# A two-layer hybrid backbone on one core: recurrence levels in blocks, and a fixed TensorE order in the second mixer

## The chip, the core and the metric

The kernel runs on one core of a Trainium2 chip. The core has TensorE (PE in the profile; PEld is its loading of weights), VectorE (DVE), ScalarE (ACT), GpSimd (POOL) and SyncE (SP), which issues most DMAs. They share SBUF; matrix products go to PSUM, a small memory of eight banks that ACT and DVE empty. The metric is device time in microseconds, the median of several runs.

## What is computed

Two transformer-like layers over 512 latent tokens and 256 context tokens, of width 1024. Each layer has a mixer and a gated feed-forward network, each between norms that are scaled and shifted by a conditioning vector. The mixers hold a gated linear recurrence in both directions, and this is what the change is about:

```python
def _chunk_gla(q, k, v, g, s0):
    # S_t = diag(exp(g_t)) S_{t-1} + k_t v_t^T,  o_t = S_t^T q_t
    ...
def _directional_scan(q, k, v, g, n_ctx, reverse):
    o_ctx, s_ctx = _chunk_gla(seg(q, c_sl), seg(k, c_sl), seg(v, c_sl), seg(g, c_sl), s0)
    o_lat, _ = _chunk_gla(seg(q, t_sl), seg(k, t_sl), seg(v, t_sl), seg(g, t_sl), s_ctx)
```

The first mixer (`even_mixer`) has four heads of 64 keys and 128 values, for context and latents, beside an attention. The second (`odd_mixer`, HGRN2) has eight heads of 128 keys and 128 values. There q is silu of a projection, the forget gate f and the key 1 - f come from a sigmoid of another projection for each direction, only the latents' outputs are needed, and the context gives no more than the two starting states. The outputs are normed by head and multiplied by silu of a gate projection.

## The kernel before

Weights come by DMA in units of 128 x 1024 (`unit`, L447 to L459), and each is split in two parts, wH (ACT, L456) and wL (DVE, L457), so that a product is three TensorE passes (`mm3`, L463: L466, L467, L468). `gemm_T` gives a projection with tokens along the free axis; `gemm_nat` gives one with tokens on partitions. Three units of raw weights and four of each split part are in flight, so loads run ahead of their use.

A recurrence is done by `scan` (from L642) without a loop over time. The tile `arr` holds four rows: key and query for one direction, key and query for the other. For block sizes b = 1, 2, 4, ... 64 one level does this: ACT copies the halves that this level needs from `arr` to `qk` (L698, one copy of 128 x 1024 for both directions), DVE multiplies the running decays into one half of `arr` for each direction (L713, twice), and DVE forms the decays of the next level (L714). For b up to 16 a call of `compact` follows each copy: 16 small products of 32 x 32 blocks (`pc`, L675; 32 for the first mixer's longer pieces), which DVE merges by a mask into `CT` (L687). Before the levels one `compact` does the diagonal (evacuated by ACT, L685). Levels 32 and 64 give products of 64 x 64 blocks (`pb`, L731), which ACT copies to `ST` (L739) and DVE completes from `CT` (L742). Then, for each direction, the keys are transposed (`knp`, L757) and copied (`kn`, L758), multiplied with the values (`pd`, L762), and three updates give the states at the tile borders (L768, L770). Last come the output products (`po`, L784) and their evacuation by a function of the caller.

The first mixer calls `scan` in `gla_job` for two pairs of heads, each for the context and for the latents, in a list of steps (`"q kv qk0 v0 c0 prep l0 qk1 v1 g0 c1 r0 l1"`).

In the second mixer, `prep(hd)` makes a head's operands: for each direction the product `ff` (256 context columns, then 512), the sigmoid (L1174), the gates (L1178, L1180) and keys (L1179, L1181) by DVE, a running product over the context (L1186 or L1191), and then the product `fq`. The function `state` transposes the context's keys (`kcT`, L1199), copies them (L1201), and multiplies them with the values to the starting state (`S`, L1204). Then DVE forms q, the two decayed queries and the sum of keys (L1218 to L1221). `head` runs `scan` and norms the output (L1230 to L1236). The program goes

```python
            ready = prep(0)
            for hd in range(8):
                nxt = prep(hd + 1) if hd < 7 else None
                ...
                head(hd, *ready)
```

with three of four gate products (`gate`) ahead of the last head and one behind it.

The order on each engine isn't that of the program text: a planner in the framework takes instructions by their place in the program and by when it reckons them ready, and writes one fixed order for each engine. So the small products of a head stand between the wide products of the next. `keep_in_program_order` is the call that takes an instruction out of this choice. Tiles with a tag share a ring of buffers; a tile waits until the one that held its buffer is done with. PSUM has two "mm" tiles (two banks each, for wide products), two "sc" tiles that are taken in turn (`pc`, `pb`, `pd`, `S`), and two "tr" tiles (transposes and `po`). `qk` has four buffers.

Of the kernel before, what the change touches and what calls it, by code (L numbers as in the profile page):

```python
# [133 lines left out]
class Net:  # L134
# [3 lines left out]
    def __init__(self, ctx, tc, I, out):  # L138
# [3 lines left out]
        self.whole = False  # L142
        self.turns = []
# [10 lines left out]
    def open_pool(self, name, side="left"):  # L154
        return self.tc.alloc_tile_pool(name=name, bufs=1, side=side, reuse_waits="tile")

# [41 lines left out]
    def col_rows(self, nm, r0, r1, parts):  # L198

        rows = self.wp.tile([P, WU], F32, tag="mraw", bufs=2, name=nm)[: r1 - r0, :P]  # L200
        for at, src, n in parts:
            self.nc.scalar.dma_start(out=rows[at - r0 : at - r0 + n, :], in_=src)
        pt = self.tr_tile(f"pt_{nm}")
        self.nc.tensor.transpose(pt[:, 0 : r1 - r0], rows, self.ident[0 : r1 - r0, 0 : r1 - r0])
        self.nc.vector.tensor_copy(self.col[:, r0:r1], pt[:, 0 : r1 - r0])
# [56 lines left out]
    def mod_cols(self, l, acc, n, outs):  # L262
# [6 lines left out]
        for b in range(nb):  # L269
            last = nc.tensor.transpose(pt[:, b * P : (b + 1) * P], rows[:, b * P : (b + 1) * P], self.ident)  # L270
# [10 lines left out]
    def mod_group(self, l, ms, which=None, pool=None, bufs=2):  # L281
# [5 lines left out]
        for k in range(KD):  # L287
            us = self.mod_loads(l, ms, k, pool, bufs)
            for j in range(4):
                self.nc.tensor.matmul(  # L290
# [9 lines left out]
    def mod_vec(self, pool, jobs, own=None, bufs=2):  # L300
# [7 lines left out]
        for l, ms, then in jobs:  # L308
# [19 lines left out]
            for j in range(4):  # L328
                nc.tensor.matmul(
# [28 lines left out]
    def gate_rows(self, l, m, row, streams=2):  # L358
# [7 lines left out]
        nc.tensor.transpose(pt[0:n, 0:P], gc.rearrange("p r k -> p (r k)"), self.ident)  # L366
# [28 lines left out]
    def pre_norm(self, pool, t, xt, A, B, h):  # L395
# [8 lines left out]
        def turn():  # L404
            for hf in range(2):
# [3 lines left out]
                for kk in range(4):  # L409
                    k = hf * 4 + kk  # L410
                    nc.tensor.transpose(pt[:, kk * P : (kk + 1) * P], xn[:, k * P : (k + 1) * P], self.ident)
# [51 lines left out]
    def mm3(self, out, stat, mov, first, last):  # L463

        mm = self.nc.tensor.matmul
# [86 lines left out]
    def seven(self, W, h, X, fill, then=None):  # L552
# [5 lines left out]
        for wn, hn, x in SEVEN:  # L558
# [5 lines left out]
            for k in range(4):  # L564
                for i, (a, b) in enumerate(((wH, hH), (wH, hL), (wL, hH))):
                    nc.tensor.matmul(  # L566
# [75 lines left out]
    def scan(self, pool, nm, arr, q, ksum, dscale, f, nt, hpp, V, Sf0, Sb0, final, o_evac):  # L642
# [25 lines left out]
        def compact(lhs, rhs, m):  # L668
            for hh in range(hpp):
                pc = self.sc_tile(f"pc{nm}")  # L670
                pv = pc[:, : nt * 32].rearrange("p (s i) -> p s i", s=nt)
                for t in range(nt):
                    for j in range(4):
                        cs = slice(t * P + 32 * j, t * P + 32 * j + 32)
                        nc.tensor.matmul(  # L675
                            pv[32 * j : 32 * j + 32, t, :],
                            lhs[rowp(hh), cs],
                            rhs[rowp(hh), cs],
                            start=True,
                            stop=True,  # L680
                            tile_position=(rowt(hh), 32 * j),
                        )
                dst = CT[:, hh * nt : (hh + 1) * nt, :]
                if m is None:
                    nc.scalar.mul(dst, pv, dscale)  # L685
                else:
                    nc.vector.copy_predicated(dst, self.masks[:, m, :][:, None, :].to_broadcast([P, nt, 32]), pv)  # L687

        compact(ksum, q, None)

        b = 1
        while b < P:
            qk = pool.tile([P, 2, N], F32, tag="qk", bufs=4, name=f"qk{nm}{b}")
            src = arr[:, 0, :]
            inap = bass.AP(
                tensor=src.tensor, offset=src.offset, ap=[src.ap[0], [N, 2], [2 * b, N // (2 * b)], [2 * N + b, 2], [1, b]]
            )
            nc.scalar.copy(qk.rearrange("p a (n h o) -> p a n h o", h=2, o=b), inap)  # L698
# [5 lines left out]
            blk = arr.rearrange("p a (n h o) -> p a n h o", h=2, o=b)  # L704
            nb = N // (2 * b)
            tv = f[:, :, : 2 * nb].rearrange("p a (n h) -> p a n h", h=2)
            for lo, ohalf, thalf in ((0, 0, 1), (2, 1, 0)):
                dst = blk[:, lo : lo + 2, :, ohalf, :]
                tb = tv[:, :, :, thalf]
# [11 lines left out]
        for hh, t0, n in groups:  # L721
# [3 lines left out]
            for i in range(n):  # L725
                T0 = (t0 + i) * P
                for K, Q, x in ((K64, Q64, 1), (K32, Q32, 0)):
                    for j in range(2):
                        rs = slice(T0 + 64 * j, T0 + 64 * j + 64)
                        c0 = 64 * (j ^ x)  # L730
                        nc.tensor.matmul(  # L731
# [12 lines left out]

        states = [{}, {}]
        ends = []
        for d, S0, a in ((0, Sf0, 0), (1, Sb0, 2)):
            order = list(range(nt)) if d == 0 else list(range(nt))[::-1]
            steps = order if final else order[:-1]
            order = order + [None]  # L750
            kn = pool.tile([P, len(steps), P], F32, tag="kn", bufs=1 if hpp > 1 else 2, name=f"kn{nm}{d}")
            prev = S0
            if prev is not None:
                states[d][order[0]] = prev
            pt = self.tr_tile(f"knp{nm}{d}")
            for i, t in enumerate(steps):
                nc.tensor.transpose(pt[:, i * P : (i + 1) * P], arr[:, a, t * P : (t + 1) * P], self.ident)  # L757
            nc.scalar.copy(kn, pt[:, : len(steps) * P].rearrange("p (s i) -> p s i", s=len(steps)))  # L758
            pd = self.sc_tile(f"pd{nm}{d}").rearrange("p (s v) -> p s v", s=4)
            for i, t in enumerate(steps):  # L760
                for hh in range(hpp):
                    nc.tensor.matmul(  # L762
# [10 lines left out]
            ends.append(prev)  # L773

        for hh, t0, n in groups:
            po = self.tr_tile(f"po{nm}").rearrange("p (s v) -> p s v", s=4)
            for t in range(t0, t0 + n):
# [5 lines left out]
                for i, (l, r) in enumerate(terms):  # L783
                    nc.tensor.matmul(po[:, t - t0, :], l, r, start=(i == 0), stop=(i == len(terms) - 1))  # L784
            o_evac(hh, t0, n, po[:, :n, :])
        return ends


    def even_mixer(self, h, mix, zu, last):
# [32 lines left out]
        for g in range(0, NTT, 4):  # L822
            pt = self.tr_tile("zTp")
            n = min(4, NTT - g)
            for i in range(n):
                nc.tensor.transpose(pt[0:32, i * P : (i + 1) * P], zn[:, g + i, :], self.ident)
# [90 lines left out]
    def gla_gates(self, mixg, tp, c, zT, wg):  # L917
# [4 lines left out]
        for t0, N in ((SEQ, CTX), (0, SEQ)):  # L922
            f = mixg.tile([P, 2, N], F32, tag=f"glaf{c}{t0}", bufs=1, name=f"glaf{c}{t0}")
            for d in range(2):
                bias = self.col[:, R_BG + 2 * d + c : R_BG + 2 * d + c + 1]
                pt = self.sc_tile(f"logit{c}{d}", 1)[:, :N]
                nc.tensor.matmul(pt, wg[:, d, c * P : (c + 1) * P], zT[:, t0 : t0 + N], start=True, stop=True)
# [712 lines left out]
```

## Time and profile before

| | |
|---|---|
| median of three runs | 1818.79 us (1816.62 to 1823.14) |
| profiled execution, device time | 1825.62 us |
| its span, first to last instruction | 1823.7 us |
| granted TensorE clock, mean | 0.983 |
| busy PE / DVE / ACT / POOL | 97% / 73% / 45% / 3% |
| recurrences of the first mixer | 138.6 to 279.5 us |
| second mixer up to its gated output | 1087.5 to 1405.4 us |

The profile is of one execution. A row of a group names the line of the kernel, the engine, the operation, the tile written and those read, the shapes, how often, the busy time and the mean of one. Matmul ends are modelled, and matmuls overlap, so the distance between two starts tells more than a duration. A row of waits says which instruction of which line waited for what: total, times, longest. "issue" means that nothing which the profile shows was waited for. One product of 32-bit operands that aren't split appears as two matmuls. Tile names of the two mixers' scans end in g and h (`pcg`, `pch`).

### The profile page before, as it was taken

The numbers are of one execution on the slowest core, as the hardware profiler recorded it, in microseconds if no ns is written. First come the engines' busy times: TensorE is split into PE (matmuls) and PEld (weight loads), VectorE is DVE, ScalarE is ACT, GpSimd is POOL, SyncE is SP. The second block draws the span as 40 slices with busy tenths as digits, with TensorE's granted clock in tenths as the row PEclk, the third lists the DMA queues.
The fourth block names the chain that finished last, engine by engine and source line by source line (L and its number), as shares of the span: only waits on it lengthen the run. The fifth ranks groups of instructions, "written<-read, shape, count | busy, mean of one in ns | idle before, by whom it ended". The sixth has DMA issues, their size and how long they took to land. (4 is left out here: it accounts for less than half of the span.)

```text
span 1823.7 us, 33154 instructions
## 1 busy us (share of the span) xinstructions
PE 1764.6 (97%) x13864; PEld 1556.4 (85%) x13864; DVE 1322.6 (73%) x2163; ACT 826.7 (45%) x1362; POOL 55.2 (3%) x73
## 2 busy tenths in 40 slices
PE   6999999999999999999999999999999999999998
PEld 4897985887898879898998898888899899999897
DVE  5757756874787999796676516777775587878885
ACT  5614436763743233233335624544544564434442
POOL 1001100000000000000000100000000000000000
PEclk8999988999999999999999999999999999999999
DMA  8631013014343456452214322112113333333333
GB/s 312 193 116 53 7 43 105 13 36 139 115 139 104 141 182 197 149 163 62 66 58 162 116 70 71 36 48 59 37 50 103 129 97 110 106 103 93 93 105 127
DMA packets 169586, 187.26 MB, mean 103 GB/s; under 512 B 6198, under 2 KB 140892, under 8 KB 169436
## 3 DMA queue, kind: packets, MB, share of 16 engines
q1 hardware_dynamic: 167504, 181.56, 32.0%
q10 hardware_dynamic: 1932, 3.59, 0.6%
q8 instruction: 108, 1.77, 0.4%
q14 instruction: 42, 0.34, 0.1%
HBM read 175.66 MB, written 9.46 MB: 102 GB/s over the span
## 5 line engine op out<-in xcount | busy, mean ns | idle before, releaser
L457 DVE TENSOR_TENSOR wL<-raw,wH 128x1024 fp32r<-128x1024 f32 (+1 forms) x126 | 151.0, 1206 | 132.1 <-ACT wH L456 131.8
L511 ACT CAST wH<-raw 128x1024 fp32r<-128x1024 f32 x120 | 124.6, 1051 | 189.5 <-PE acc L468 62.4
L456 ACT CAST wH<-raw 128x1024 fp32r<-128x1024 f32 (+1 forms) x126 | 129.0, 1039 | 175.6 <-PE ff L467 57.3
L512 DVE TENSOR_TENSOR wL<-raw,wH 128x1024 fp32r<-128x1024 f32 x120 | 145.3, 1221 | 64.1 <-ACT wH L511 63.8
L466 PE MATMUL nat<-wH,x 128*128 128x256 f32 (+1 forms) x608 | 177.7, 292 | 0.0
L467 PE MATMUL nat<-wL,x 128*128 128x256 f32 (+1 forms) x608 | 177.4, 292 | 0.0
L468 PE MATMUL nat<-wH,x 128*128 128x256 f32 (+1 forms) x608 | 176.3, 290 | 0.0
L466 PE MATMUL acc<-wH,gH 128*128 128x512 f32 x440 | 173.3, 394 | 0.0
L468 PE MATMUL acc<-wH,gL 128*128 128x512 f32 x440 | 172.8, 393 | 0.0
L467 PE MATMUL acc<-wL,gH 128*128 128x512 f32 x440 | 172.7, 393 | 0.0
L604 DVE TENSOR_TENSOR y<-y,acc 128x1024 f32<-128x1024 f32 x135 | 114.9, 862 | 30.8 <-PE acc L468 28.8
L322 DVE SCALAR_TENSOR_TENSOR macc<-mraw,scT,macc 128x1024 f32<-128x1024 f32 x98 | 123.0, 1277 | 6.9 <-DMA mraw<-in_mod_w_dram 6.7
L467 PEld LDWEIGHTS nat<-wL,x 128*128 128x128 f32 x608 | 119.1, 196 | 2.4 <-issue 1.8
L466 PEld LDWEIGHTS nat<-wH,x 128*128 128x128 f32 x608 | 119.0, 196 | 2.3 <-issue 1.7
L468 PEld LDWEIGHTS nat<-wH,x 128*128 128x128 f32 x608 | 119.0, 196 | 1.8 <-issue 1.1
L384 POOL TENSOR_TENSOR rs<-ms,neghalf 128x1 f32<-128x1 f32 (+2 forms) x62 | 53.4, 861 | 1753.1 <-DVE ms L382 1712.6
L466 PEld LDWEIGHTS acc<-wH,gH 128*128 128x128 f32 x440 | 82.5, 188 | 20.1 <-issue 0.8
L468 PEld LDWEIGHTS acc<-wH,gL 128*128 128x128 f32 x440 | 82.5, 187 | 18.8
L467 PEld LDWEIGHTS acc<-wL,gH 128*128 128x128 f32 x440 | 82.5, 188 | 17.6
L467 PE MATMUL ff<-x,wH 128*128 128x256 f32 (+1 forms) x256 | 89.0, 348 | 0.0
L466 PE MATMUL ff<-x,wH 128*128 128x256 f32 (+1 forms) x256 | 87.9, 343 | 0.6 <-issue 0.6
L698 ACT COPY qkh<-arr 128x1024 f32<-128x1024 f32 x56 | 62.9, 1134 | 51.6 <-DVE arr L713 48.3
(348 smaller groups left out, 4522.2 us busy)
## 6 DMA issues: line engine op xcount, KB each, us to landing
mraw<-in_mod_w_dram SPq DMA_DIRECT2D x96, 512.0 KB, 4.6
raw<-in_ffn_w_gate_dram SPq DMA_DIRECT2D x44, 512.0 KB, 4.2
raw<-in_ffn_w_up_dram SPq DMA_DIRECT2D x44, 512.0 KB, 3.8
raw<-in_ffn_w_down_dram SPq DMA_DIRECT2D x44, 512.0 KB, 3.7
raw<-in_odd_w_in_dram SPq DMA_DIRECT2D x40, 512.0 KB, 3.9
raw<-in_even_w_in_dram SPq DMA_DIRECT2D x16, 512.0 KB, 4.9
x<-xr SPq DMA_DIRECT2D x14, 512.0 KB, 2.7
xr<-x SPq DMA_DIRECT2D x14, 512.0 KB, 3.2
```

Of the source, the lines that this page charges most:

```text
L322: nc.vector.scalar_tensor_tensor(a, u, w, a, op0=ALU.mult, op1=ALU.add)
L384: nc.gpsimd.tensor_tensor(rs, ms, self.neghalf.to_broadcast([P, w]), op=ALU.pow)
L456: nc.scalar.copy(H[:, :m], raw[:, :m])
L457: nc.vector.tensor_tensor(L[:, :m], raw[:, :m], H[:, :m].bitcast(F32), op=ALU.subtract)
L466: mm(out, stat[0], mov[0], start=first, stop=False)
L467: mm(out, stat[0], mov[1], start=False, stop=False)
L468: mm(out, stat[1], mov[0], start=False, stop=last)
L511: self.nc.scalar.copy(H, f)
L512: self.nc.vector.tensor_tensor(L, f, H.bitcast(F32), op=ALU.subtract)
L604: nc.vector.tensor_tensor(y, y, pt, op=ALU.add)
L698: nc.scalar.copy(qk.rearrange("p a (n h o) -> p a n h o", h=2, o=b), inap)
```

## The change

- `scan` becomes a generator that yields between its stages. In a level the copy is made by direction: ACT copies one direction's half (128 x 512), DVE multiplies it, then the same for the other.
- `compact` takes a list of levels. The diagonal and levels 1, 2 and 4 are done as one block of products into one "sc" tile after level 4; levels 8 and 16 as another after level 64. The merges into `CT` stay one for each level.
- The transposes and copies of the keys for both directions come ahead of both `pd` products (`kn` has two buffers in the first mixer also).
- In the second mixer the keys (`kc`, `arr`) and the square of the output move from DVE to ACT; the context's transposes and starting states of both directions are grouped, with one "sc" tile for the two states.
- All TensorE calls go through `mm` and `tr`, which keep program order while `self.pinned` is set: during the heads and gates of the second mixer. The order there is written out by hand with generators; head `hd`'s products, the scan of head `hd - 1` and the output products of head `hd - 2` take turns. The gate products are spread over the last recurrence.
- The first mixer runs the same generator to its end in `gla_job`, and its order stays with the planner.

```diff
@@ scan
-        def compact(lhs, rhs, m):
+        def compact(levels):
             for hh in range(hpp):
-                pc = self.sc_tile(f"pc{nm}")
-                pv = pc[:, : nt * 32].rearrange("p (s i) -> p s i", s=nt)
...
+                pc = self.sc_tile(f"pc{nm}")[:, : len(levels) * nt * 32]
+                pv = pc.rearrange("p (l s i) -> p l s i", l=len(levels), s=nt)
...
-            nc.scalar.copy(qk.rearrange("p a (n h o) -> p a n h o", h=2, o=b), inap)
             qks[b] = qk
-            if b <= 16:
-                compact(qk[:, 0, :], qk[:, 1, :], {1: 0, 2: 1, 4: 2, 8: 3, 16: 4}[b])
...
+            for lo, half in ((0, 0), (2, 1)):
+                dst = blk[:, lo : lo + 2, :, half, :]
+                nc.scalar.copy(qkv[:, :, :, half, :], dst)
...
                 nc.vector.tensor_tensor(dst, dst, tb, op=ALU.mult)
             nc.vector.tensor_tensor(f[:, :, :nb], tv[:, :, :, 0], tv[:, :, :, 1], op=ALU.mult)
+            if b == 4:
+                yield
+                compact([(ksum, q, None)] + [(qks[x][:, 0, :], qks[x][:, 1, :], m) for m, x in enumerate((1, 2, 4))])
             b *= 2
         tot = f
+        yield
+        compact([(qks[x][:, 0, :], qks[x][:, 1, :], m) for m, x in ((3, 8), (4, 16))])
...
@@ odd_mixer
-                    nc.vector.tensor_scalar(kc, sg[:, SEQ:], nlb1, lb1, op0=ALU.mult, op1=ALU.add)
+                    nc.scalar.activation(kc, sg[:, SEQ:], AF.Identity, bias=lb1, scale=nlb1)
...
-                    nc.vector.tensor_scalar(arr[:, 2 * d, :], sg[:, :SEQ], nlb1, lb1, op0=ALU.mult, op1=ALU.add)
+                    nc.scalar.activation(arr[:, 2 * d, :], sg[:, :SEQ], AF.Identity, bias=lb1, scale=nlb1)
...
-                    nc.vector.tensor_tensor(sq, o, o, op=ALU.mult)
+                    nc.scalar.activation(sq, po, AF.Square)
...
+            go = lambda x: next(x, None)
+            self.pinned = True
+            outs = scan = iter(())
             for hd in range(8):
-                nxt = prep(hd + 1) if hd < 7 else None
...
+                given = []
+                new = prep(hd, given)
+                go(scan)
...
```

For one head the written order reads, with the TensorE work of each turn in brackets: scan [none: levels 1, 2, 4], new [ff of direction 0, 256 columns], outs [po], new [ff of direction 0, 512], new [ff of direction 1, 256], scan [first block], new [ff of direction 1, 512], new [fq], scan [second block, pb, knp of both directions], new [kcT], scan [pd], new [S]. For the end it reads: scan, gate 0, outs [po], gate 0, gate 1, scan [first block], gate 1, gate 2, gate 2, scan [second block, pb, knp], gate 3, scan [pd], gate 3, scan [po], gate 3 (its two multiplications with the output).

More of the change, by code (lines that the diff above doesn't have):

```diff
@@ L772, in scan @@
                 states[d][order[i + 1]] = S
-            ends.append(prev)
+            if ends is not None:
+                ends.append(prev)
+        yield
         for hh, t0, n in groups:
@@ L956, in evac @@
             nc.scalar.copy(gv[:, t0 + t : t0 + t + n, (2 * c + hh) * P : (2 * c + hh + 1) * P], po)
-        s0 = states or (None, None)
-        return self.scan(gp, nm, arr, q, k, 2.0, f, nt, 2, V, s0[0], s0[1], t0 >= LT, evac)
+        ends = [] if t0 >= LT else None
+        for _ in self.scan(gp, nm, arr, q, k, 2.0, f, nt, 2, V, states, ends, evac):
+            pass
+        return ends
     def gated_T(self, pool, src, nh, grow, cat, groups):
```

231 lines of the change are left out of this document (141 added, 90 removed).

## The prediction

> **What bounds the kernel now.** First the page: the span, the busy shares of the engines, and the queue that carries instructions.
>
> ```profile
> span 1823.7 us, 33154 instructions
> ...
> PE 1764.6 (97%) x13864; PEld 1556.4 (85%) x13864; DVE 1322.6 (73%) x2163; ACT 826.7 (45%) x1362; POOL 55.2 (3%) x73
> ...
> q8 instruction: 108, 1.77, 0.4%
> ```
>
> TensorE (PE) is busy almost throughout, so only what PE does or waits for can move the end. A busy PE isn't a full PE, though: I read next the table by stretches, of PE alone, for the stages that the change touches, and two pieces of them (the first head's products, and a piece with small products).
>
> ```profile
> core 0: us, PE busy (x), PEclk, DMA share, GB/s
> 1087.53:1109.66 22.13, 22.13 (x122) 1.00 0.34 96
> 1169.60:1175.11 5.51, 4.53 (x192) 1.00 0.35 98
> 138.60:175.20 36.60, 32.48 (x561) 0.91 0.18 50
> 175.20:279.50 104.30, 101.14 (x1533) 0.92 0.09 27
> 1087.50:1133.40 45.90, 45.87 (x254) 1.00 0.28 81
> 1133.40:1338.70 205.30, 200.00 (x2390) 1.00 0.16 48
> 1338.70:1405.40 66.70, 66.42 (x930) 1.00 0.23 73
> ```
>
> The second mixer fills 45.9 + 205.3 + 66.7 = 317.9 us: two heads' products, then six heads at 205.3 / 6 = 34.2 us each (each with the next head's products in it), then the last two recurrences with the gate products. In the six heads PE is idle for only 5.3 us. In the first mixer's recurrences it is idle for 4.1 us in the first stretch and 3.2 us in the rest. So all idle time together is some 13 us (0.7% of the span): the change can't win much by shorter chains alone. The view of waits says what ends the idle time (us in total, times, longest), the second mixer's first, then two entries of the first mixer's recurrences.
>
> ```profile
> PE pch L675 <- issue: 3.8, 4, 1.4
> PE ff L466 <- issue: 0.6, 1, 0.6
> PE poh L784 <- DVE Sh L770: 0.5, 3, 0.2
> ...
> PE pcg L675 <- issue: 0.5, 1, 0.5
> ...
> PEld pcg L675 <- issue: 4.2, 7, 1.8
> ```
>
> In the second mixer hardly anything waits for VectorE (DVE) or ScalarE (ACT): the largest entry is "issue", where PE waits for nothing that the profile shows, in the middle of the small products. The rest of what a head loses is in the timeline, where wide products (ff) and small ones (pch) alternate.
>
> ```profile
> 1136.26 0.90 PE L675 MATMUL pch<-qkh 128*32 128x32 f32 x64
> 1137.09 0.39 PE L466 MATMUL ff<-x,wH 128*128 128x256 f32 x1
> 1137.31 0.28 PE L467 MATMUL ff<-x,wH 128*128 128x256 f32 x1
> 1137.43 0.28 PE L468 MATMUL ff<-x,wL 128*128 128x256 f32 x1
> ...
> 1137.91 0.28 PE L466 MATMUL ff<-x,wH 128*128 128x256 f32 x1
> 1138.12 0.46 PE L675 MATMUL pch<-qkh 128*32 128x32 f32 x32
> 1138.51 0.39 PE L467 MATMUL ff<-x,wH 128*128 128x256 f32 x1
> ```
>
> Wide products start 0.12 us apart (1137.31 to 1137.43), but 0.22 after a small block (1137.09 to 1137.31), and the small block starts 0.21 after the last wide one. Each stretch of wide products between small ones costs 0.2 us more than its work.
>
> **The change part by part.** Five terms.
>
> *1. Fewer stretches (gain).* In the head that begins at 1133.4 I count eight stretches of wide products between small blocks; the fixed order leaves three (before the output products, after them up to the first block of levels, and from there to the second block). Five fewer at 0.2 us are 1.0 us a head, 6 us in six heads. With the gate products 16 stretches become 5: 2.2 us. Sum **-8.2**. The Trainium skill, page "TensorEngine Tiling (Array Packing)", section "Key Properties", says that a change of tiling mode drains TensorE; the 0.2 us agree with it in kind, and it gives no price.
>
> *2. Idle "issue" time in the second mixer.* 27728 matmuls and loads over 108 packets are 257 instructions a packet, so I take that queue to feed PE. From 1169.60 to 1175.11 PE got through 192 matmuls and as many loads in 5.51 us and stood idle for about 1 us with no wait: 257 instructions in 3.7 us (an estimate from these rows). One level is 32 matmuls in 0.39 us (1138.12 to 1138.51), so the new first block of four levels is 128 matmuls and 128 loads in 1.6 us. If a packet ends at its start, PE waits for 3.7 - 1.6 = 2.1 us; if the boundary lies in the wide products, not at all. It has to fall within some 60 of 256 instructions around the block's start: a quarter of seven heads at a mean of 1 us gives 1.9 us, against 4.4 now: **-2.5** (ends: -4.4, and 7 x 2.1 - 4.4 = +10.3). On the other side stands a rule of the Trainium skill, page "Runtime: NRT & Kernel Launch", section "Instruction fetch mechanics": instructions come in blocks of 256, and crossing a boundary is mostly hidden. By that there would be no such idle time after the change, here or in term 5; the 3.8 us above don't agree with it.
>
> *3. New waits that the fixed order makes (loss).* The order ends each head with small things alone: second block, pbh, knph, kcT, pdh, S. Two of them need a PSUM buffer that ACT or DVE has yet to empty, and no wide product may step in. These are the rows of before for the same steps.
>
> ```profile
> 1144.29 1.15 PE L731 MATMUL pbh<-qkh 128*64 128x64 f32 x32
> 1145.38 0.87 PE L757 MATMUL knph<-ident,arr 128*128 128x128 f32 x6
> 1145.49 0.59 ACT L739 COPY STh<-pbh 128x512 f32<-128x512 f32 x1 [0.87 <-PE pbh L731]
> 1145.97 0.87 ACT L758 COPY knh<-knph 128x384 f32<-128x384 f32 x2
> 1146.01 0.47 PE L467 MATMUL ff<-x,wH 128*128 128x512 f32 x1
> 1146.56 1.56 PE L762 MATMUL pdh<-y,knh 128*128 128x128 f32 x12
> 1147.67 0.34 DVE L770 SCALAR_TENSOR_TENSOR Sh<-S,f,pdh 128x128 f32<-128x128 f32 x1
> 1148.56 0.34 DVE L770 SCALAR_TENSOR_TENSOR Sh<-Sh,f,pdh 128x128 f32<-128x128 f32 x1
> 1149.42 0.34 DVE L770 SCALAR_TENSOR_TENSOR Sh<-Sh,f,pdh 128x128 f32<-128x128 f32 x1
> ```
>
> kcT (L1199) takes the "tr" buffer of knph's first direction (two buffers, both just written). Its copy ends half of 0.87 us after 1145.97, at 1146.4 to 1146.5; knph ends at 1146.01, so kcT waits 0.5 us, and its second part, for the second copy, 0.2 more: 0.7 us. Behind it wait pdh and S. The products S (L1204) take the "sc" buffer of pdh's first direction, which is free after that direction's three state updates. Low end: back to back, 3 x 0.34 = 1.0 plus some 0.15 to start, less pdh's second half (0.7): 0.45 us. High end: spaced as in before, where multiplies came between them, 1147.67 to 1149.76 = 2.1, plus 0.15, less 0.7: 1.5 us. I take 1.1, near the high end, since DVE stays loaded. In seven heads 7 x (0.7 + 1.1) = 12.6, and 0.5 for head 0, whose S has only its own copies to wait for: **+13.1** (ends 8.6 and 15.9). Behind S waits the next head's first product, and with it all PE work. I looked for others: the first block comes 2.9 + 2.5 + 5.4 + 2.9 us of PE work after those steps (24 products at 0.12, the output products, 24 at 0.227, 24 at 0.12; 48 x 0.12 + 72 x 0.227 is the 22.13 us of one head's products above), the second 48 x 0.227 = 10.9 us after the first, so the level chain (below) is ready in both; the weights' DMAs and splits run a head ahead in SP's queue as now.
>
> *4. ACT and DVE work, and the mixer's end.*
>
> ```profile
> L698 ACT COPY qkh<-arr 128x1024 f32<-128x1024 f32 x42 | 47.1, 1134 | 37.8 <-DVE arr L713 36.2 <-PE pch L675 1.1
> L739 ACT COPY STh<-pbh 128x512 f32<-128x512 f32 x6 | 3.5, 587 | 1.1 <-PE pbh L731 0.9
> L713 DVE TENSOR_TENSOR arr<-arr,f 128x512 f32<-128x512 f32 x84 | 56.2, 688 | 7.7 <-ACT qkh L698 5.9
> L1181 DVE TENSOR_SCALAR arr<-sg,nlb,lb 128x512 f32<-128x512 f32 x12 | 6.5, 541 | 0.0
> L1179 DVE TENSOR_SCALAR kc<-sg,nlb,lb 128x256 f32<-128x256 f32 x12 | 4.9, 408 | 0.0
> L1232 DVE TENSOR_TENSOR sq<-y 128x512 f32<-128x512 f32 x6 | 4.1, 691 | 0.0
> L415 ACT ACTIVATE f<-hT,modcol,aff 128x128 f32<-128x128 f32 x80 | 30.3, 488 | 3.0 <-PE hT L411 3.0
> L1479 ACT ACTIVATE xT<-xT,modcol,aff 128x512 f32<-128x512 f32 x6 | 4.7, 809 | 1.8 <-DVE aff L1470 1.8
> ```
>
> Seven copies of 1.13 (7.9 us) become 14 of half the size, 0.59 by the nearest row: 8.2. A level's chain falls from 1.13 + 2 x 0.69 = 2.5 us to about 0.59 + 2 x 0.69 = 2.0, as the second copy runs beside the first multiply. DVE loses 2 x 0.54 + 2 x 0.41 + 0.69 = 2.6 us a head, and ACT gains 2 x 0.81 + 2 x 0.6 (between 0.49 and 0.81) + 0.6 = 3.4. In 34 us of a head neither becomes the bound, and PE, the bound, issues the same products: **0**. If the cover went, the seven levels' gain of 7 x 0.5 us is what the chain has in reserve. At the end, 4.6 us of wide products that now follow the last recurrence (1400.8 to 1405.4, from the timeline) come before it, so its evacuation, three elementwise steps of 0.6 to 0.7 us for the first output operand, stands open: **+1** (0 to 4.6).
>
> *5. First mixer (its order isn't fixed).* The first chain's idle 4.1 us shrink by up to 7 x 0.3 (its tiles are half as wide): **-2** (0 to -4). Four jobs lose about four stretches each: 16 x 0.2 = **-3.2**. But a long job's first block is now 256 matmuls and 256 loads in 2.8 us with nothing between, so one packet at least is used up inside it: 2.1 us and a part of a second, 2.7 for each of two jobs, and 0.5 for each of the short ones: 6.4, against 2.5 now (between the 0.5 and 4.2 of the waits): **+3.9** (ends -2.5 and +8).
>
> The sum: -8.2 - 2.5 + 13.1 + 0 + 1 - 2 - 3.2 + 3.9 = **+2.1 us**. It is worked out on the profiled execution (span 1823.7, device time 1825.6, which holds some 2 us around the span). That one lies 6.8 us above the median of the three runs, 1818.8; I add the difference to the median: **1821 us**, no change that can be told.
>
> **The rivals.**
>
> A, faster: *the fixed order waits little*. The updates run back to back and the copies come at once (0.45 + 0.45 instead of 1.8 in seven heads: -6.3), and no block waits for instructions in the first mixer (-3.9): 1811. For it: DVE has 2.6 us a head less to do, and the updates are older in the program than the next head's levels. Against it: the two buffers are the same as before, and in before the updates were spaced by 0.9 us. A part of A (0.08) is that waits for instructions vanish and the rest stays as forecast: -1.9 - 6.4: 1813. The Trainium skill's page "Runtime: NRT & Kernel Launch" (section as in term 2) would have it so.
>
> B, slower: *instructions run short*. Place: the first block of levels. Price: up to 2.1 us a head and not 0.5; if the boundary lies badly in all seven heads, +12.8: 1834. It decides once more than about four heads are hit. For it: 1.4 us is already the longest wait with three wide products between levels. Against it: the boundary moves on from head to head, and the wide products on both sides refill.
>
> C, slower: *DVE's and ACT's queues stand in the way of the buffers*. When the second block is done, q's three multiplies and the sum for ks (4 x 0.69) may be first in DVE's queue, then the block's two merges, four STh copies, and a multiply of the next head's levels between each two updates; the next head's first copies (0.6 each) may go ahead of knph's on ACT. Price: 0.6 more for kcT, 1.0 more for S: 7 x 1.6 = 11 us: 1832. It decides where both waits pass 2.3 us a head. For it: PE can't step aside any more. Against it: DVE's share falls.
>
> **How the numbers follow.** 0.3% (5.5 us) is about what a measurement of this kernel can tell from no change. Forecast, within that: 0.34. A: 0.28. B: 0.16, C: 0.22. So faster 0.28, same 0.34, slower 0.38. The range reaches from A with the first chain's other 2 us and 5 of the 6.8 us that A leaves of term 3, to C or B with the tail's upper end: 1804 to 1838. The forecast's own range is 1813 to 1824.
>
> **What would show it.** Right: in the six heads' stretches PE idles before kcT (released by ACT's knh copy) and before S (by DVE's updates), 0.7 and 1.1 us, at about 34 us a head as now; three stretches of wide products in a head; no PE idle time ended by qk copies; "issue" waits at pcg in the first mixer larger than now. Wrong: a head below 33 us (A), idle "issue" time in the pch blocks of most heads (B), waits at S of 2 us and more (C), or PE waiting for level copies at the second block, which I hold for covered by 10.9 us of products.

## The result, and the profile after

The changed kernel takes 1828.61 us (median of 8 runs, 1825.04 to 1835.94); the kernel before takes 1819.28 us on the same chip (8 runs, 1812.77 to 1823.7). The ratio is 1.0062, with a 95% interval of 1.0045 to 1.0078. So it is slower by 0.6%: within the predicted range, 8 us above the predicted 1821, and past the 0.3% that the forecast ("no change that can be told") had set itself. The profiled execution took 1833.68 us. The ratios below leave out one later run of the changed kernel, which took 2137.69 us at a mean granted clock of 0.748.

First the page of the changed kernel: the span and the queue that carries instructions, nearly as before.

```profile
span 1831.9 us, 33164 instructions
...
q8 instruction: 109, 1.79, 0.4%
```

Then the table by stretches, TensorE alone, of both kernels, cut at the same events: the first small product of the first mixer, the first transpose of its output (`catT`), the first `ff` of the second mixer, the first `catT` after it, the end. The rows of the first mixer, the second and what follows it are shown. Columns: length, PE busy (matmuls), granted clock, DMA share, GB/s. Before:

```profile
139.60:396.20 256.60, 244.72 (x3034) 0.93 0.13 39
...
1087.50:1405.40 317.90, 312.29 (x3571) 1.00 0.20 58
1405.40:1823.70 418.30, 403.68 (x2658) 0.99 0.35 107
```

After:

```profile
138.60:383.90 245.30, 235.84 (x3034) 0.96 0.13 41
...
1075.60:1408.65 333.05, 310.62 (x3571) 0.98 0.18 52
1408.65:1831.90 423.25, 404.01 (x2658) 0.99 0.35 108
```

The change of 8.2 us in the span is the sum of parts with opposite signs: the first mixer is 11.3 us shorter, the second 15.1 us longer, the stretch behind it 5.0 us longer; what lies ahead of the first mixer and between the two makes up the rest (-0.6). The prediction had -1.3 for the first mixer, +2.4 for the second and +1 behind it. Its total is near by luck: two misses partly cancel. A second profile of the changed kernel (span 1825.5 us, taken with the run e13_changed_again below) has 244.1, 333.0 and 418.1 us for these three stretches. So the two mixers come out again, and the 5.0 us behind them do not.

What PE waits for in the second mixer after the change (total, times, longest):

```profile
PE S L165 <- DVE Sh L789: 14.4, 7, 2.1
PE pdh L165 <- DVE CTh L705: 5.0, 7, 0.7
PE kcT L168 <- ACT knh L769: 1.8, 7, 0.3
PE S L165 <- ACT kcn L1240: 1.2, 1, 1.2
```

These are the new waits of the fixed order, 22.4 us. The prediction had named those at `S` and `kcT`, but not the 5.0 us at `pd`. The "issue" entries of before are gone. One head's end in the timeline of PE:

```profile
1307.71 0.87 PE L168 MATMUL knph<-ident,arr 128*128 128x128 f32 x6
1308.85 0.82 PE L168 MATMUL kcT<-ident,kc 128*128 128x128 f32 x4 [0.26 <-ACT knh L769]
1310.38 1.60 PE L165 MATMUL pdh<-y,knh 128*128 128x128 f32 x12 [0.72 <-DVE CTh L705]
1314.03 1.13 PE L165 MATMUL S<-y,kcn 128*128 128x128 f32 x8 [2.04 <-DVE Sh L789]
1314.92 0.48 PE L165 MATMUL ff<-x,wH 128*128 128x256 f32 x2
```

And the same microseconds on DVE:

```profile
1308.84 0.68 DVE L1229 TENSOR_TENSOR arr<-q,f 128x512 f32<-128x512 f32 x1
1309.44 0.68 DVE L1230 TENSOR_TENSOR arr<-q,f 128x512 f32<-128x512 f32 x1
1310.04 0.29 DVE L705 COPY_PREDICATED CTh<-masks,pch 128x128 f32<-128x128 uint8 x1
1310.28 0.69 DVE L723 TENSOR_TENSOR arr<-arr,f 128x512 f32<-128x512 f32 x1
1310.89 0.91 DVE L757 COPY STh<-CTh 32x128 f32<-32x128 f32 x4
1311.82 0.35 DVE L789 SCALAR_TENSOR_TENSOR Sh<-S,f,pdh 128x128 f32<-128x128 f32 x1
1312.09 0.69 DVE L723 TENSOR_TENSOR arr<-arr,f 128x512 f32<-128x512 f32 x1
1312.69 0.34 DVE L789 SCALAR_TENSOR_TENSOR Sh<-Sh,f,pdh 128x128 f32<-128x128 f32 x1
1312.95 0.68 DVE L724 TENSOR_TENSOR f<-f 128x512 f32<-128x512 f32 x1
1313.55 0.34 DVE L789 SCALAR_TENSOR_TENSOR Sh<-Sh,f,pdh 128x128 f32<-128x128 f32 x1
```

The merge at 1310.04, behind q's multiplies, frees the buffer that `pd` takes (1310.38). The first update (1311.82) starts when four STh copies are done, the next two stand behind a multiply each; when the third is done, S gets its buffer (1314.03). Nothing on DVE is late by itself; the queue's order is what PE waits for, and no wide product may step in.

One thing was in no term of the sum. Here is the granted clock (the column behind the brackets) in three heads: from the wait at S on in the first row, and right after S, where 24 `ff` products of 256 columns follow, in the other two:

```profile
1276.10:1280.50 4.40, 3.38 (x19) 0.71 0.00 0
1314.92:1319.38 4.46, 4.46 (x27) 0.62 0.02 4
...
1205.60:1208.55 2.95, 2.95 (x27) 1.00 0.00 0
```

The last two rows hold the same products of two heads: 2.95 us at full clock, 4.46 us when the clock is halved for a part of it. A mean of 0.62 over 4.46 us is 2 x 0.38 x 4.46 = 3.4 us at half clock, and the trace's record of the clock has 3.41 us. That happened in four of the seven heads with a wait at S, and costs 1.5 us each. In the second profile of the changed kernel it is four heads again, at the third, fourth, sixth and seventh of these waits and not the second, fourth, fifth and sixth, with waits of 2.04 or 2.05 us in all seven. So the kernel makes such a stretch likely, and does not fix where it falls.

### The profile page after: what moved, and what is told of

The parts are those of the page before. It is cut to its first block, busy times and chain, and to the rows that moved or that the text cites. A ratio compares the mean times of both kernels' runs of the same rounds, so it can differ in the third digit from the quotient of the medians.

```text
span 1831.9 us, 33164 instructions
## 1 busy us (share of the span) xinstructions
PE 1755.6 (96%) x13864; PEld 1555.8 (85%) x13864; DVE 1308.9 (71%) x2123; ACT 857.1 (47%) x1486; POOL 55.1 (3%) x73
## 5 line engine op out<-in xcount | busy, mean ns | idle before, releaser
L165 PE MATMUL nat<-wH,x 128*128 128x256 f32 (+1 forms) x1216 | 229.4, 288 | 1.6 <-issue 1.6
L165 PEld LDWEIGHTS nat<-wH,x 128*128 128x128 f32 x1216 | 193.6, 193 | 3.0 <-issue 2.6
L165 PE MATMUL ff<-x,wH 128*128 128x512 f32 (+1 forms) x512 | 132.6, 350 | 0.0
L165 PE MATMUL oproj<-wH,x 128*128 128x512 f32 x320 | 101.9, 396 | 0.4 <-DVE x L439 0.2
L165 PEld LDWEIGHTS ff<-x,wH 128*128 128x128 f32 x512 | 91.8, 200 | 9.9
L165 PE MATMUL ff<-x,wL 128*128 128x256 f32 (+1 forms) x256 | 88.5, 346 | 0.0
L718 ACT COPY qkh<-arr 128x512 f32<-128x512 f32 x112 | 69.4, 636 | 34.7 <-DVE arr L723 29.0
```

The lines of the kernel that those rows point to most:

```text
L165: return self.pin(self.nc.tensor.matmul(*a, **k))
L718: nc.scalar.copy(qkv[:, :, :, half, :], dst)
```

## The experiments

Each time is told as a ratio to the kernel before on the same chip.

**Which part does it?** Two kernels split the change by mixer: one gives the new recurrence to the first mixer alone (the second is that of before), one has everything but that.

```diff
 gla_job
-        return self.scan(gp, nm, arr, q, k, 2.0, f, nt, 2, V, s0[0], s0[1], t0 >= LT, evac)
+        for _ in self.scan2(gp, nm, arr, q, k, 2.0, f, nt, 2, V, states, ends, evac):
```

> The first mixer as after the change, the second mixer as before. Theory (the change gains in the first mixer, by fewer stretches and shorter chains, and loses more than that in the second mixer's fixed order): 8 to 12 us under the kernel before, since the profiled runs reach the first kT transposes 15 us and the second mixer 12 us earlier after the change. Rival (those 12 us are chance, the granted clock having been 0.95 against 0.92 in that stage of the two profiled runs): within 4 us of before. The blind forecast's terms for the first mixer gave 1 us.

> The second mixer as after the change, the first mixer as before. Theory: 13 to 18 us over before, since the second mixer took 333.0 us after the change against 317.9 before, and its end 2 us more. Rival (the first mixer's gain is chance): 9 us over before, as the whole change.

First mixer only: 0.9928 (0.9914 to 0.9942), 13 us faster. Second mixer only: 1.0093 (1.008 to 1.0106), 17 us slower. Together that is +0.2%, beside +0.6% for the whole (and +0.5% in the repeat below): the parts nearly add up, and the rest is about the size of the intervals. So two opposite effects are real, one in each mixer. A third kernel keeps all the work, and gives the second mixer's order back to the planner:

```diff
-            self.pinned = True
+            self.pinned = False
```

> The change with self.pinned left False: the same instructions, the same program text, and the planner orders TensorE. Theory (the fixed order makes the waits before kcT, pd and S): the waits of some 3.8 us a head shrink to under 1, and the second mixer comes back to 318 us or less: 1804 to 1814. Rival (the loss is in the work itself: keys and squares on ACT, copies by halves, so the level chain or ACT is late whatever the order): 1825 and more.

0.9862 (0.9848 to 0.9876), 25 us faster than before. Its second mixer by stretches:

```profile
1073.80:1376.30 302.50, 302.35 (x3569) 1.00 0.20 57
```

PE idles for 0.15 us in it, against 22.4 us after. The same products, copies and blocks: the loss is the order alone.

**Where in the order?** One edit gives the starting states the other PSUM ring, so that S needn't wait for the updates.

```diff
-                pS = self.sc_tile("S0")
+                pS = self.tr_tile("S0")
```

> The change with one word altered: the starting states' products take a tr tile of PSUM and not an sc tile, so they needn't wait until DVE's state updates have emptied pd's. Order and work stay. Theory: the wait of 2.0 to 2.4 us before S goes in seven heads (15 us), and with it most of the four stretches at half clock that follow it (1.5 us each): 1806 to 1816. If the half clock is not a matter of that wait: 1813 and the stretches stay. Rival (DVE is late, and whoever needs it next waits as long): the wait moves to po or pd, and the time stays within 4 us of the change's.

0.9913 (0.99 to 0.9925), 16 us faster than before. The head's end:

```profile
1289.80 0.82 PE L168 MATMUL kcT<-ident,kc 128*128 128x128 f32 x4 [0.26 <-ACT knh L769]
1291.34 1.60 PE L165 MATMUL pdh<-y,knh 128*128 128x128 f32 x12 [0.71 <-DVE CTh L705]
1292.78 1.06 PE L165 MATMUL S<-y,kcn 128*128 128x128 f32 x8
```

S follows `pd` at once, the two small waits stay, and no clock is halved in the heads. The second mixer takes 311.1 us (1072.5 to 1383.6), 21.9 less than after, though the waits at S were 14.4 us. The difference, 7.5 us, is about the halved clock, 4 x 1.5 = 6 us. Whether the wait really causes that was tried with useless work: nine products that nothing reads (18 matmuls) fill the wait, and the changed kernel was timed once more beside it.

```diff
+                for i in range(9 if hd else 0):
+                    self.mm(pq[:, 512:640], self.ident, fi[:, LT, hd * P : (hd + 1) * P], start=True, stop=True)
                 pS = self.sc_tile("S0")
```

> The changed kernel with useless work added: ahead of the starting states S of heads 1 to 7 stand nine more 128x128 products (18 matmuls at about 0.11 us, 2.0 us) into an unused part of the head's fq tile, which nothing reads; the wait before S was 2.2 us. Theory (TensorE's clock is halved after a few us with little work, and the wait is the cause): S starts as late as before, no half-clock stretch is left in the heads, and the kernel gets 4 to 9 us faster than the changed kernel although TensorE has 14 us more work. Rival (the half-clock stretches have another cause, the small products or chance): they stay, and the time is that of the changed kernel or up to 3 us above it.

> The changed kernel itself once more, on the same chip as the kernel with the filler and the two others: 1.0062 of before again (1.0045 to 1.0078), with three to five half-clock stretches in the second mixer's heads.

With the filler 1.0009 (0.9994 to 1.0024), the changed kernel 1.0049 (1.0031 to 1.0067): 0.4% or 7 us faster with 14 us more work on TensorE. One head of the kernel with the filler in the timeline:

```profile
1299.11 1.60 PE L165 MATMUL pdh<-y,knh 128*128 128x128 f32 x12 [0.69 <-DVE CTh L705]
1300.55 2.17 PE L165 MATMUL fq<-y,ident 128*128 128x128 f32 x18
1302.80 0.46 PE L165 MATMUL S<-y,kcn 128*128 128x128 f32 x2
```

and its second mixer by stretches:

```profile
1068.90:1395.90 327.00, 318.66 (x3696) 1.00 0.18 54
```

S starts 3.7 us after `pd` (1302.80 - 1299.11) as it did after the change (1314.03 - 1310.38), but the clock stays at 1.00, and the mixer takes 327.0 us, 6.0 less than 333.0. So it is the idle time that leads to the halved clock, at this place, and the price of a wait of 2 us was up to 3.5 us.

Is a fixed order bad as such? Another one, also written out by hand, puts S behind the next head's first two wide products, and wide products ahead of each step that needs a buffer:

```diff
+                outs, scan, old = scan, head(hd, *given[0]), new
+            for x in (scan, g[0], old, outs, g[0], scan, g[1], g[1], scan, g[2], scan, g[2], scan, g[3], g[3]):
+                go(x)
```

(a head then reads: ff of direction 0, both parts; S of the head before; po; first block; ff of direction 1; second block, pb and knp; fq; kcT; pd).

> Another order written out by hand, fixed as in the changed kernel, with the same work: a head's starting states S come after the next head's first two wide products, the output products and the first block are put behind them, and wide products stand ahead of the second block. Theory (the loss is made by small products that need a buffer at a place where nothing else may step in; a fixed order as such costs nothing): S never waits more than 0.3 us, no stretch at half clock in the heads, head period 32 to 33.5 us, time 1797 to 1806 on the scale of 1824.9 for the kernel before, beside 1800 for the order left to the planner. Rival (a fixed order always meets some wait, and a wait removed comes back elsewhere): a new idle time of 1 us or more a head, at the keys' transposes, pd or the output products, 1808 to 1820.

0.9848 (0.9825 to 0.987): 28 us faster than before, the lowest ratio of all. Its second mixer, and the end of a head:

```profile
1074.10:1372.30 298.20, 298.20 (x3571) 1.00 0.21 63
```

```profile
1249.59 0.39 PE L165 MATMUL fq<-x,wL 128*128 128x512 f32 x1
1249.82 0.60 PE L168 MATMUL kcT<-ident,kc 128*128 128x128 f32 x4
1250.26 1.50 PE L165 MATMUL pdh<-y,knh 128*128 128x128 f32 x12
1251.52 0.48 PE L165 MATMUL ff<-x,wH 128*128 128x256 f32 x2
```

PE is busy for the whole of the mixer: the waits did not come back elsewhere in it, and the rival falls. Behind the mixer one new wait did come:

```profile
PE oproj L165 <- ACT x L438: 3.6, 1, 3.6
```

The planner's order and this one can't be told apart by their times (the intervals meet).

**Why does the first mixer gain 13 us?** One kernel makes the level copies by direction and leaves the small products level by level; another makes the blocks and leaves one copy a level. Both change the first mixer alone.

```diff
 copies only, in each level
+            if b <= 16:
+                compact([(qk[:, 0, :], qk[:, 1, :], {1: 0, 2: 1, 4: 2, 8: 3, 16: 4}[b])])
 blocks only, in each level
-                nc.scalar.copy(qkv[:, :, :, half, :], dst)
+            nc.scalar.copy(qk.rearrange("p a (n h o) -> p a n h o", h=2, o=b), inap)
```

> Kernel before, with a first mixer whose level copies are made by direction but whose small products follow level by level as before. The second mixer is that of before. With both parts the first mixer gave 13.1 us. Theory (blocks save stretches, copies by direction shorten the chain of levels where PE waits): the copies give the smaller part, 2 to 5 us: ratio 0.997 to 0.999. Rival (the gain is the shorter chain, blocks add only waits for instructions): 8 to 13 us or more, ratio 0.993 to 0.9955.

> Kernel before, with a first mixer whose small products come in blocks of levels but whose level copy stays one for both directions. The second mixer is that of before. Theory (blocks save stretches): 8 to 11 us, ratio 0.994 to 0.9957. Rival (the gain is the shorter chain): 0 to 4 us, ratio 0.998 to 1.0.

Copies only: 0.9944 (0.9924 to 0.9964), where the rival had it. Blocks only: 0.9959 (0.9945 to 0.9973), at the edge of where the theory had it (0.994 to 0.9957). So the one gives 10 us and the other 7, where both parts together give 13. The difference is about what the intervals allow, and the parts aren't cleanly split: both kernels also have the third part of the change, the keys' transposes ahead of both `pd` products with two `kn` buffers. No run has that part alone, so what each of the three is worth by itself stays open. The stretch of before's first table row in the three kernels (copies only, blocks only, both):

```profile
140.00:383.60 243.60, 233.31 (x3035) 0.97 0.14 41
```

```profile
139.40:386.30 246.90, 234.74 (x3034) 0.96 0.14 41
```

```profile
140.20:381.10 240.90, 231.15 (x3034) 0.99 0.14 42
```

Beside before's 256.60 with 244.72 busy at 0.93: idle time falls little (11.9 us before; 10.3, 12.2 and 9.8), busy time falls by 10 to 14 us for the same matmuls, and the granted clock rises in all three. A mean of 0.93 over 256.6 us is 2 x 0.07 x 256.6 = 36 us at half clock; the others have 15, 20 and 5. At 1.5 us lost in each 3.41 this is worth 9, 7 and 14 us (an estimate). I count 83 changes between the recurrence's products and others in before's timeline there, 71 with copies only and 55 in the other two, worth 1 to 3 us at 0.2 a stretch. Each of these clocks is of one execution, and with the same new recurrence the stretch is at 0.96 and at 0.98 in the two profiles of the changed kernel, so they do not rank the three kernels. The timed runs, each listed with its mean clock, say it over more executions. In 57 of the kernel before, from 1828.55 us at 0.984 to 1810.42 us at 0.991, a line through all falls by 15 us for each 0.01 of clock. The estimate makes that 16 us: 0.01 of 1820 us is 36 us at half clock. The runs with the whole new first mixer have 0.989 on average where before has 0.9845, worth 7 of the 13 us; copies only 6 of 10, blocks only 7 of 7. So about half of this gain or more is clock, by the estimate; no run here varied the clock of the first mixer alone.

**What makes the second mixer fast when the order is free?** Two tries: keys and squares back on DVE, with the order free; and the new recurrence put into the kernel before, with nothing else changed in the second mixer.

```diff
 order free, keys on DVE (the query's key row and the square likewise)
-                    nc.scalar.activation(kc, sg[:, SEQ:], AF.Identity, bias=lb1, scale=nlb1)
+                    nc.vector.tensor_scalar(kc, sg[:, SEQ:], nlb1, lb1, op0=ALU.mult, op1=ALU.add)
 new recurrence in the order of before
-                self.scan(gp, f"h{hd}", arr, q, ks, 1.0, f, LT, 1, V, S0[0], S0[1], False, evac)
+                for _ in self.scan2(gp, f"h{hd}", arr, q, ks, 1.0, f, LT, 1, V, S0, None, evac):
+                    pass
```

> The changed kernel without the fixed order (the planner chooses in the second mixer), and with the keys and the square of the output back on DVE. With these on ACT that kernel was at 0.9862 of before. Theory (moving this work to ACT is worth nothing, as neither engine is the bound): 0.985 to 0.988. Rival (DVE's updates free the buffers earlier with less work on DVE, and the gain comes from there): 0.990 to 0.994, with waits at S or kcT.

> The new recurrence (copies by direction, blocks) in both mixers, everything else as in the kernel before: the second mixer's program order, the planner's choice, keys and squares on DVE. Beside it stand the run with the new recurrence in the first mixer alone (13.1 us faster than before) and the whole change without the fixed order (24.9 us faster). Theory (in the second mixer too the blocks and copies give the gain, by fewer stretches and no waits for instructions): 20 to 25 us faster than before, ratio 0.986 to 0.989. Rival (that gain needs the new program order or the work moved to ACT): 11 to 15 us faster, ratio 0.992 to 0.994.

Keys on DVE: 0.9881 (0.9858 to 0.9904), not to be told from 0.9862. Its second mixer takes 302.6 us against 302.5: with the order free, the work moved to ACT is worth nothing. New recurrence with the program order of before: 0.9974 (0.9961 to 0.9987), 5 us faster and 8 slower than with the second mixer left alone: less than even the rival gave it. Its timeline shows why. With that program the planner puts both blocks of a head together, 192 products in a row, and in four heads PE stops in their midst for no wait of the kernel's (behind these rows, the stretch of the whole second mixer):

```profile
1161.45 0.26 PE L165 MATMUL pch<-qkh 128*32 128x32 f32 x4 [3.30 <-issue]
...
1198.02 0.53 PE L165 MATMUL pch<-qkh 128*32 128x32 f32 x19 [2.65 <-issue]
...
1235.29 0.74 PE L165 MATMUL pch<-qkh 128*32 128x32 f32 x35 [3.07 <-issue]
...
1272.80 0.95 PE L165 MATMUL pch<-qkh 128*32 128x32 f32 x50 [3.17 <-issue]
```

```profile
1073.60:1401.70 328.10, 311.44 (x3570) 0.96 0.19 58
```

The mixer takes 25.6 us more than with the free order: 16.7 us of idle time, 12.2 of it in the four stops, and a clock of 0.96, worth some 11 us by the estimate above.

The stops come with 4, 19, 35 and 50 of the 192 products left: after product 188, 173, 157 and 142, 15 to 16 earlier from head to head. A head is 398 matmuls and as many loads, 796 instructions; three packets of 256 are 768; 28 instructions or 14 matmuls a head is what the packets' ends would move by, close to what is seen. In the heads without a stop the pair of ends, 128 products apart, doesn't fall into the block (the fifth in this row would have 126 and -2). To test this, 64 matmuls of 32 columns were put ahead of the second mixer, which move all ends by 64 products:

```diff
+            pz, self.side = self.sc_tile("pz"), 1 - self.side
+            [nc.tensor.matmul(pz[:, :32], self.ident, self.ident[:, :32], start=True, stop=True) for _ in range(32)]
             ready = prep(0)
```

> The kernel with the new recurrence in both mixers and the order of before in the second, with 64 more matmuls of 32 columns ahead of the second mixer (about 2 us of work that nothing reads); the order on TensorE is otherwise the same. There each head's 192 products in one block wait 2.9 to 3.5 us for instructions in heads 2 to 5, at product 188, 173, 157 and 142: steps of 15 to 16, as a head is 796 instructions and three packets are 768. Theory (a wait comes when two ends of packets, 128 products apart, fall into one block): 64 matmuls move the ends 64 products forward, so heads 2 to 5 are free and waits of about 3 us come in head 1 near product 140 and in heads 6 and 7 near 190 and 174: three instead of four, 3 to 6 us faster than without the shift, ratio 0.994 to 0.997. Rival (the wait belongs to the block, whatever stands before it): the same four heads wait, same time or 2 us more.

```profile
1131.99 0.80 PE L165 MATMUL pch<-qkh 128*32 128x32 f32 x52 [2.83 <-issue]
...
1300.65 0.27 PE L165 MATMUL pch<-qkh 128*32 128x32 f32 x2 [2.67 <-issue]
...
1338.33 0.48 PE L165 MATMUL pch<-qkh 128*32 128x32 f32 x17 [2.78 <-issue]
```

The four heads are free, and the stops come in the heads that were named, at 140, 190 and 175 (named: 140, 190, 174). So two packet ends in one block make the stop, in this mixer. They are not the whole condition. In the first mixer of the kernel without the shift a run of 242 products of 32 columns (235.74 to 238.75 us) is long enough for two ends 128 products apart at most of the places where they can fall, and PE has no "issue" wait in it. The DMA share was 0.02 there, and 0.32 to 0.39 in the seven stretches with stops; whether the transfers matter, no run here tested.

The time missed what was expected: the ratio is 1.0021 (1.0007 to 1.0036), not 0.994 to 0.997, and above the 0.9974 of the kernel without the shift, though in the profile the second mixer is 4.5 us shorter (323.6 for 328.1). Half of this is the 64 added matmuls, which were reckoned at 2 us and held PE for 8.8:

```profile
1069.17:1078.01 8.84, 8.84 (x67) 0.79 0.42 119
```

That leaves 4.3 us lost, of the 8.5 between the two ratios. The rest stays open: the two kernels were timed on different chips, beside other runs of before.

## Why the prediction was right or wrong

*Term 1, fewer stretches (-8.2): right in size.* The kernel with S on the other ring keeps the fixed order and shows no halved clock in the heads: PE is busy for 303.16 us in its second mixer, against 312.29 before, 9.1 less. The timelines also have the forecast's 41 fewer stretches of wide products (changes between `ff`, `fq`, `nat` and all else: 133 before, 51 now). But the free order has 109 of these changes and is busy for only 302.35 us. What it shares with the written order is 32 changes between full tiles (128*128 in the rows) and narrow ones (128*32, 128*64), against 82 before. So that the gain is 0.2 us for each of the stretches that the term counted isn't shown.

*Term 2, "issue" (-2.5): right in sign, too small.* The whole 4.4 us went, its low end. The reasoning behind it was off: a first block of 128 products is one packet of 256 instructions, so it holds one end, and no stop was seen in it in any of the kernels that keep it apart. The stops seen in the kernel with 192 products in a row come when two ends fall into one block, and cost 2.65 to 3.3 us, not 2.1. Rival B's "the boundary moves on from head to head" was true by only 15 products, so several heads in a row are hit. It didn't decide here since the written order keeps the two blocks apart.

*Term 3, new waits (+13.1): the failed step in the second mixer.* The waits at `S` and `kcT` and their releasers were right, the sizes weren't, and one place was missing: 22.4 us of waits, and 6 us of halved clock behind four of them. S waited 2.06 us a head and not 1.1. The updates are 0.87 us apart, as the high end (1.5) had it; but the first starts some 0.4 us later than taken, behind the STh copies (0.16 us ahead of `pd`'s end at 1311.98, where the high end has 0.55), and S 0.14 after the third is done. `kcT` waits 0.26 and not 0.7. `pd` waits 0.71 for a merge that stands behind q's multiplies, which the term didn't hold. On DVE this is rival C's mechanism: its queue stands in the way. On ACT it isn't, since C had `kcT` wait longer than the forecast. C's condition for the waits at `kcT` and S, more than 2.3 us a head, is just met (2.3; 3.0 with `pd`'s), and so is the prediction's own sign of being wrong, waits at S of 2 us and more; a head took 36.4 us (S at 1132.32 and, six heads on, at 1350.94), not about 34. The forecast had DVE's falling share of busy time against C, and what counts is what DVE has *queued ahead* of an update. The changed kernel's 1828.61 lies between the forecast and C's 1832 only because term 5 was off the other way. Rival A, which trusted short waits, is refuted by 14.4 us at S.

*Term 4, ACT, DVE and the end: right for the work, somewhat low for the end.* Moving the keys is worth nothing; the level copies made no wait in the second mixer. Behind the mixer the waits at `catT` grew from 0.4 us to 2.8 and, in the second profile, 2.9: 2.4 us or so, not 1. The whole stretch was 5.0 us longer in the first profile and 0.2 shorter in the second, so the rest of the 5.0 isn't shown to come from the change.

*Term 5, first mixer (-1.3): the failed step there; -11.3 measured, and 13 us by the kernel that has this part alone.* Idle time fell by 2.4 us (taken: 2), and 28 fewer changes of kind are 14 stretches (taken: 16). The instructions' price was too high. The weight loads of `pcg` after the change:

```profile
PEld pcg L165 <- issue: 5.5, 9, 1.7
```

That is 1.3 more than the 4.2 of before, where 3.9 was taken. What was missing is the clock: 0.91 and 0.92 stood in the PEclk column of the two rows that the prediction quoted of this mixer, and no term priced them. After the change the mean is 0.96, worth about 7 us by the estimate above (0.98 in the second profile).

## What to carry to other kernels

When an order on TensorE is fixed, place wide products ahead of each step that must wait for a PSUM buffer, and read the queue of the engine that frees it entry by entry; between two orders with the same work the right places were worth 35 us of this mixer's 333 (333.0 to 298.2). A granted clock below 1 in a stretch is a term of its own: it can mean that short waits there cost more than their length, and that shortening them gains more. A gain that a change has in one stage and loses in another is seen only by splitting the kernel by stage, as the total showed 0.6%.

## What the runs showed of the hardware

A wait of some 2 us, with only small products for 4 us ahead of it, can halve TensorE's clock for 3.41 us, which costs another 1.5 us; it did so in four heads of seven in both profiles of the changed kernel, and in none when the idle time was filled. The Trainium skill, page "TensorE: Matmul & The Clock Gate", section "What's actually happening", has a window of 3413 ns that runs free of the kernel, and the length agrees. Its section "Why this matters for your kernels" warns of idle gaps over about 3 us; here gaps of 2.0 us at S were enough. Which heads are spared changes from one execution to the next, as a window that runs free would have it; no run here tested that.

TensorE's instructions come in packets of about 256 (27728 matmuls and loads in 108 packets before), and in the second mixer two ends of packets within some 2 us of small products stopped it for 2.65 to 3.3 us, seven times in two kernels; in the first mixer a run of the same kind was not stopped. The page "Runtime: NRT & Kernel Launch" of the Trainium skill, section "Instruction fetch mechanics", has the 256, which the steps of 15 to 16 products come near to (14 by this count), and calls the crossing mostly hidden; the stops above are not.
